# Low weight parts of the last five weight groups: formed by GpSimd in two steps instead of by VectorE in one

## The chip, the cores and the metric

The kernel runs on one core of one Trainium2 chip. The metric is the device time of one execution in microseconds. A profile of one execution shows what TensorE (PE), VectorE (DVE), ScalarE (ACT), GpSimd (POOL) and the transfer queues did.

## The reference

One encoder layer over 1024 tokens of width 1024, a grid of 16 rows by 64 columns. Cut to what matters here:

```python
h = _rmsnorm(x, norm_gain[l])
proj = h @ w_in[l]                                     # 13 groups of 256 columns
q_a, k_a, v_a, g_a, q_b, k_b, v_b, g_b = jnp.split(proj, split_at, axis=-1)
o_a = _gqa_blocked(q_a, k_a, v_a) * jax.nn.silu(g_a)   # 8 heads over all 1024 keys
o_b = _neighbourhood_attn(q_b, k_b, v_b, na_rpb[l])    # window 8 x 16, learned bias
o_b = o_b * jax.nn.silu(g_b)
x = x + jnp.concatenate([o_a, o_b], axis=-1) @ w_out[l]  # 4 more groups of 256 columns
return _rmsnorm(x, final_norm_gain)
```

## The kernel before

Everything is float32 in the reference; TensorE multiplies float16. So each operand is split into a high part (the float16 rounding) and a low part (the rest, float16 too), and a product takes three matmuls: high by high, high by low, low by high.

The weights come in 17 groups of 1024 x 256: 0 to 12 from the input projection (11 and 12 are the gate of the neighbourhood attention), 13 to 16 from the output projection. A group is loaded by a transfer that GpSimd issues (`load_w`, L212) into one of two buffers `raw`; ScalarE squares it in four quarters of 128x512 (L362); a tiny TensorE sum (L378), a VectorE step (L380) and a power on GpSimd (L381) make its scale, a column of `sm`. Then `split(g)` forms the parts, again by quarters: `hi` on ScalarE (L404, `raw` times the scale, rounded to float16) and `lo` on VectorE (L409, `raw` times the scale minus the high part). After the fourth `lo` the group counts as ready, and the load of group g + 2 into the same buffer is put on GpSimd's queue.

The program is written out slot by slot by a planner, `Flow`. One slot is one unit of attention: scores, softmax and, some slots later, the product with the values. Work beside it (evacuations, splits) waits as jobs of ScalarE and VectorE with a cost and a lateness, and each slot takes as many jobs as its budget of that engine allows (`work`). TensorE's own order takes a fixed number of projection matmuls per slot (`fill`). What is written is what each engine executes, in order: an instruction whose input is late holds everything behind it on its engine.

There are two stretches of attention. In the second, the neighbourhood attention (from about 370 us to 510 us of the span; the program marks it by `late["b"]`), there are 32 slots, four for each of the eight blocks u of 128 queries in the order 0, 7, 1, 2, 3, 4, 5, 6. In a slot TensorE writes two score tiles into two of three banks (L815, L818), VectorE adds the bias and takes the maximum (L836, tile `nm` holds the maxima), ScalarE takes the exponential twice and makes the high part (L838, L840), VectorE the low part (L845), and a transpose by DMA follows. Groups 12 to 16 are split in this stretch.

Other steps that the prediction speaks of, all in this stretch or at its border:

- The gate of the first attention: ScalarE writes tanh to `th` (L694; the only buffer of that kind, used by the second gate too), GpSimd scales it (L702), VectorE and GpSimd multiply (L703, L704). For the second gate VectorE alone reads `th` (L699).
- `narrow` (L786) on GpSimd adds the window's mask to the bias of one head, for the blocks 1 to 6, eight times in all.
- Evacuation of the values: VectorE writes `qkg` (L877, one buffer), GpSimd multiplies it into the mixed output (L879).
- The scaling of a finished block (`os`): sums on ScalarE and VectorE (L902, L907), a power on GpSimd (L910), then the high part on ScalarE (L915) and the low part on VectorE (L919), a transpose, and the output projection, whose result VectorE adds to x (L976), reloaded by transfers that GpSimd issues (L966).

Of the kernel before, what the change touches and what calls it, by code (L numbers as in the profile page):

```python
# [12 lines left out]
OP = mybir.AluOpType  # L13
# [34 lines left out]
class Flow:  # L48
# [13 lines left out]
    def at(self, delay, pos, fn, *a):  # L62
        self.due.setdefault((self.slot + delay, pos), []).append((fn, a))

    def job(self, eng, cost, fn, *a, delay=1, late=1, key=None):

        self.jobs.append((late, self.slot + delay, self.number(), eng, cost, fn, a, key))
# [75 lines left out]
def kernel(ctx: ExitStack, tc: tile.TileContext, x: bass.AP, w: bass.AP, wo: bass.AP,  # L143
# [3 lines left out]
    act, dve, pool, pe, sp = nc.scalar, nc.vector, nc.gpsimd, nc.tensor, nc.sync  # L147
# [11 lines left out]
    at, job = fl.at, fl.job  # L159
# [46 lines left out]
    raw, wp, late, x2 = {}, {}, {}, {}  # L206
# [40 lines left out]
    S_, RC, EC = 0, 17, 34  # L247
# [5 lines left out]
    def col(i, n=1):  # L253
        return sm[:, i:i + n]
# [78 lines left out]
    def alloc_wp(g):  # L333
        if g == 13:
            wp[g] = tuple(t[:, :2048].rearrange("p (k c) -> p k c", c=GC) for t in late["r"])
            return
        if g < 15:
            t = whl.tile([P, 2, KC, GC], F16, tag="whl", name=f"whl{g}")
        else:
            if g == 15:  # L340
                late["w"] = one.tile([P, 2, 2, KC, GC], F16, tag="hT0", name="whl15")
            t = late["w"][:, g - 15]
        wp[g] = (t[:, 0], t[:, 1])
# [54 lines left out]
    def split(g):  # L398

        alloc_wp(g)  # L400

        def hi(i):
            q = QUARTERS[i]
            act.activation(wp[g][0][:, q], raw[g][:, q], AF.Copy, scale=col(S_ + g))  # L404
            job("dve", 1.0 if "b" in late else 0.72, lo, i, delay=0, late=0.5 if g > 11 else 2, key=g)

        def lo(i):
            q = QUARTERS[i]
            dve.scalar_tensor_tensor(wp[g][1][:, q], raw[g][:, q], col(S_ + g), wp[g][0][:, q], op0=OP.mult, op1=OP.subtract)  # L409
            if i < 3:  # L410
                return
            ready.add(g)
            prep_e(g)
            if g + 2 < 17:
                at(1, "pre", load_w, g + 2)
            if g > 14:
                t = wraw.tile([P, 2, 1024], F32, tag="raw", name=f"x2{g}")
                for i in range(2):
                    have_x2(ORDER[2 * g - 26 + i], t[:, i])
        for i in range(4):  # L420
            job("act", 0.3 if g == 14 else 0.6, hi, i, late=0.5 if g > 11 else 2, key=g)
# [3 lines left out]
    def prep_e(g):  # L425
        dve.reciprocal(col(RC + g), col(S_ + g))
        if g < 13:
            dve.tensor_scalar(col(RC + g), col(RC + g), col(GXI), None, op0=OP.mult)
        if g in (KVA, QA, QA + 1):
            t = col(EC + g)  # L430
            dve.reciprocal(t, col(RC + g))
            dve.tensor_tensor(t, t, t, op=OP.mult)
            dve.tensor_scalar(t, t, EPS, None, op0=OP.mult)
        if g >= GATE and g < 13:
            dve.tensor_scalar(col(G2 + g - GATE), col(RC + g), 0.5, None, op0=OP.mult)
        if g == KB + 1:
            fin_scales()
        if GB <= g < 13:
            vfac(g - GB)
# [126 lines left out]
    def qa_gen(hh, up):  # L566
        def evac(pt):
            g = QA + hh
            stg = slot("stg1", [P, 2, 4, P], F16)
            a, b = (0, D) if hh == 0 else (D, 0)  # L570

            def fin(q):
                d = 4 if hh else 2
                at(d, "pre", lambda: act.activation(stg[:, :, :, a:a + D], q, AF.Copy))
                at(d, "mid", lambda: dve.tensor_tensor(stg[:, :, :, b:b + D], q, stg[:, :, :, a:a + D], op=OP.subtract))

                def tr():
                    sp.dma_start_transpose(qTa[hh][:, 2 * up:2 * up + 2].rearrange("p i h t -> p (i h) t"),
                                           stg.rearrange("p i a b -> p (i a b)"))
                at(d, "post", tr)  # L580
            norm_rope(g, up, pt, 4, 0, fin)
        yield from proj_pair(QA + hh, up, from_h, evac)

    def kva_gen(up):
        def evac(pt):
            both = slot("stg1", [P, 8, P], F16)
            stg, stg_l = both[:, :6].rearrange("p (i a) b -> p i a b", a=3), both[:, 6:]
            vs = pt[:, :, P:].rearrange("p a (h d) -> p a h d", d=D)
            at(1, "pre", lambda: act.activation(va[:, 2 * up:2 * up + 2, :, :D], vs, AF.Copy, scale=2.0 ** -14))

            def vlo():
                for i in range(2):
                    dve.scalar_tensor_tensor(va[:, 2 * up + i, :, v_lo], vs[:, i], 2.0 ** -14,
                                             va[:, 2 * up + i, :, :D], op0=OP.mult, op1=OP.subtract)
            at(1, "mid", vlo)

            def fin(k):
                def hi():
                    act.activation(stg[:, :, :2, :D], k, AF.Copy)
                    act.activation(stg[:, :, :2, D:], k, AF.Copy)  # L600
                at(2, "pre", hi)

                def lo():
                    for h, to in ((0, stg[:, :, 2]), (1, stg_l)):
                        dve.tensor_tensor(to.rearrange("p i (e d) -> p i e d", d=D),
                                          k[:, :, h, None, :].to_broadcast([P, 2, 2, D]),
                                          stg[:, :, h].rearrange("p i (e d) -> p i e d", d=D), op=OP.subtract)
                at(2, "mid", lo)

                def tr():  # L610
                    sp.dma_start_transpose(kTa[:, 2 * up:2 * up + 2].rearrange("p i a t -> p (i a) t"),
                                           both[:, :6].rearrange("p a b -> p (a b)"))
                    sp.dma_start_transpose(klo1[:, 2 * up:2 * up + 2], stg_l.rearrange("p a b -> p (a b)"))
                at(2, "post", tr)
            norm_rope(KVA, up, pt[:, :, :P], 2, 1, fin)
        yield from proj_pair(KVA, up, from_h, evac)
# [94 lines left out]
    def group(g, gens):  # L711

        def first(gen):
            prep(g + 1)
            yield from gen
        return [first(gens[0]) if g < 16 else gens[0], *gens[1:]]
# [221 lines left out]
    def have_x2(u, t):  # L938
        x2[u] = t
        if u in due:  # L940
            in_turn(load_x2, u)
# [104 lines left out]
    k, q = [kva_gen(up) for up in UP], group(1, [qa_gen(0, up) for up in UP])  # L1046
# [132 lines left out]
    a, b = ORDER[2:4]  # L1179
# [119 lines left out]
```

## Time and profile before

| | |
|---|---|
| median of 3 runs | 564.84 us (564.72 to 566.35) |
| the profiled execution | 566.36 us, of which the span is 564.5 us |
| mean granted TensorE clock | 0.977 |
| busy in the span: TensorE | 515.5 us (91%) |
| VectorE | 446.0 us (79%) |
| ScalarE | 367.8 us (65%) |
| GpSimd | 157.2 us (28%) |

The profiled execution is 1.86 us longer than its span, and 1.5 us longer than the median. A row of a timeline gives the start in us from the span's start, the duration, the engine, the line, the operation, what it writes and reads, and in brackets how long the engine stood idle before it and what ended that. Spans on GpSimd are rough.

### The profile page before, as it was taken

To read this page: it belongs to the slowest core of one execution; us is meant where nothing else is said; L and a number is where in the kernel's file an instruction comes from. 1 tells how busy PE (TensorE), PEld (TensorE's weight loads), DVE (VectorE), ACT (ScalarE), POOL (GpSimd) and SP (SyncE) were. 2 spreads that over 40 slices of the span, in tenths; PEclk is the share of its full clock that TensorE was granted. 3 is DMA by queue.
4 is the path that set the end of the run, shared out by engine and by line. 5 is a ranking of instruction groups with operands and counts; after the bars stand their busy time and mean duration, and the time that the engine had idled before them with its cause. 6 is when DMAs were issued, how large, how long until landed. Compare 5 with 4: busy or idle time off the path is not lost.

```text
span 564.5 us, 13778 instructions
## 1 busy us (share of the span) xinstructions
PE 515.5 (91%) x5583; PEld 402.4 (71%) x5583; DVE 446.0 (79%) x911; ACT 367.8 (65%) x583; POOL 157.2 (28%) x181
## 2 busy tenths in 40 slices
PE   2577989989999999999999999999998889998994
PEld 0456877767887555568888888887776667788883
DVE  4588788989887988778789887588987798988532
ACT  5546456958787759587696886367777568663211
POOL 2395887670000000000000022433821231224000
PEclk9979999999999999999999999999999998999998
DMA  8999549789999999998999899436586599996612
GB/s 242 220 181 234 122 71 210 125 143 191 203 228 174 175 216 193 193 187 173 211 197 180 189 165 214 129 68 132 105 188 105 117 255 230 181 154 139 215 38 75
DMA packets 244513, 95.47 MB, mean 169 GB/s; under 512 B 235489, under 2 KB 236001, under 8 KB 242530
## 3 DMA queue, kind: packets, MB, share of 16 engines
q1 hardware_dynamic: 240850, 73.89, 71.8%
q0 software_dynamic: 3312, 19.92, 12.2%
q8 instruction: 43, 0.70, 0.5%
q10 hardware_dynamic: 288, 0.79, 0.5%
q14 instruction: 20, 0.16, 0.1%
HBM read 29.56 MB, written 4.19 MB: 60 GB/s over the span
## 4 chain that ended last, share of the span: by engine, by line
PE 51%; DVE 9%; ACT 8%; issue 5%; DMA 4%; SPq 0%; POOL 0%; DVEq 0%; POOLq 0%; ACTq 0%
PE pj L494 19%; PE kb L494 7%; PE pjb L494 5%; PE s L725 4%; PE s L727 4%; ACT rq L838 3%; PE sb L494 3%; PE pv L758 3%; DMA ar<-ar 3%; PE pv L759 3%; PE pv L757 3%; ACT ar L840 3%; DVE ar L836 2%; DVE ar L845 2%; DMA x2b<-in_x_dram 1%
## 5 line engine op out<-in xcount | busy, mean ns | idle before, releaser
L494 PEld LDWEIGHTS <-hT 128*128 128x128 f16 x2112 | 204.9, 100 | 58.8 <-issue 16.2
L494 PE MATMUL pj<-whl,hT 128*128 128x256 f16 x1680 | 201.6, 278 | 20.9 <-DMA hT<-ar 7.8
L734 ACT ACTIVATE ar<-s,nm,sm 128x1024 f32<-128x1024 f32 x64 | 76.9, 1202 | 56.6 <-DVE nm L732 56.3
L732 DVE CUSTOM_DVE_ANT_0 ar<-s,sm 128x1024 bf16<-128x1024 f32 x64 | 82.0, 1281 | 33.9 <-PE s L727 33.6
L494 PEld LDWEIGHTS <-ar 128*128 128x128 f16 x768 | 74.6, 99 | 11.7 <-issue 2.6
L740 DVE TENSOR_TENSOR ar<-ar 128x1024 f16<-128x1024 f32 x64 | 79.5, 1242 | 1.4 <-ACT ar L735 1.4
L735 ACT ACTIVATE ar<-ar 128x1024 f16<-128x1024 f32 x64 | 67.6, 1057 | 2.1 <-DVE sum L764 0.3
L838 ACT ACTIVATE rq<-ar,nm 128x384 f32<-128x384 f32 (+1 forms) x64 | 34.1, 580 | 38.4 <-DVE nm L836 37.7
L494 PE MATMUL pjb<-whl,ar 128*128 128x256 f16 x408 | 47.4, 273 | 0.0
L494 PE MATMUL kb<-hT,whl 128*128 128x512 f16 x192 | 44.5, 379 | 0.0
L409 DVE SCALAR_TENSOR_TENSOR whl<-raw,sm,whl 128x512 f16<-128x512 f32 x52 | 38.7, 770 | 2.8 <-ACT whl L404 2.8
L758 PE MATMUL pv<-va,ar 128*128 128x64 f16 x384 | 40.1, 194 | 0.0
L757 PE MATMUL pv<-va,ar 128*128 128x65 f16 x384 | 40.1, 193 | 0.0
L759 PE MATMUL pv<-va,ar 128*128 128x65 f16 x384 | 39.9, 192 | 0.0
L757 PEld LDWEIGHTS <-ar 128*128 128x128 f16 x384 | 35.7, 97 | 5.5 <-issue 0.3
L758 PEld LDWEIGHTS <-ar 128*128 128x128 f16 x384 | 35.5, 97 | 5.5 <-issue 0.3
L725 PE MATMUL s<-kTa,rq 128*128 128x512 f16 x128 | 38.5, 383 | 0.4 <-ACT ar L734 0.4
L212 POOL DMA_DIRECT2D raw<-in_w_dram x11 | 6.7, 607 | 113.0 <-ACT ar L735 89.0
L845 DVE SCALAR_TENSOR_TENSOR ar<-rq,ar 128x768 f16<-128x768 f32 (+1 forms) x32 | 30.7, 959 | 7.9 <-ACT ar L840 7.5
L879 POOL TENSOR_TENSOR ar<-ar,qkg 128x256 f32<-128x256 f32 x16 | 18.5, 1157 | 65.0 <-DVE qkg L877 63.7
L759 PEld LDWEIGHTS <-ar 128*128 128x128 f16 x384 | 35.5, 99 | 0.0
L404 ACT ACTIVATE whl<-raw,sm 128x512 f16<-128x512 f32 x52 | 34.0, 709 | 1.4 <-POOL sm L381 1.4
(174 smaller groups left out, 978.4 us busy)
## 6 DMA issues: line engine op xcount, KB each, us to landing
raw<-in_w_dram POOLq DMA_DIRECT2D x11, 1024.0 KB, 7.7
raw<-in_wo_dram POOLq DMA_DIRECT2D x4, 1024.0 KB, 6.3
ar<-in_x_dram SPq DMA_DIRECT2D x7, 512.0 KB, 6.3
khh<-ar SPq DMA_DIRECT2D x16, 128.0 KB, 3.4
x2b<-in_x_dram POOLq DMA_DIRECT2D x4, 512.0 KB, 6.9
x<-in_x_dram POOLq DMA_DIRECT2D x4, 512.0 KB, 6.2
out_dram<-x2b SPq DMA_DIRECT2D x8, 256.0 KB, 4.2
out_dram<-x SPq DMA_DIRECT2D x7, 256.0 KB, 2.9
```

Of the source, the lines that this page charges most:

```text
L409: dve.scalar_tensor_tensor(wp[g][1][:, q], raw[g][:, q], col(S_ + g), wp[g][0][:, q], op0=OP.mult, op1=OP.subtract)
L494: pe.matmul(*o[0], **o[1])
L725: pe.matmul(s[:, c * 512:(c + 1) * 512], q, kTa[:, 4 * c:4 * c + 4, hh], start=True, stop=False)
L732: dve.tensor_tensor_reduce(out=hl[:, 1].bitcast(BF16), in0=s, in1=col(SHA).to_broadcast([P, 1024]), scale=col(NSA), scalar=3e38, op0=OP.ad ...
L734: act.activation(p32, s, AF.Exp, bias=nm, scale=col(SCA))
L735: at(0, "mid", lambda: act.activation(hl[:, 0], p32, AF.Copy))
L740: dve.tensor_tensor(hl[:, 1], p32, hl[:, 0], op=OP.subtract)
L757: pe.matmul(o, pt[:, kt], va[:, kt, hh, v_hi], start=kt == 0, stop=False)
L758: pe.matmul(o[:, :D], pt[:, kt], va[:, kt, hh, v_lo], start=False, stop=False)
L759: pe.matmul(o, pt[:, 8 + kt], va[:, kt, hh, v_hi], start=False, stop=kt == 7)
L838: act.activation(p32[:, e], t[:, e], AF.Exp, bias=nm, scale=-1.0)
L845: dve.scalar_tensor_tensor(hl[:, 1], p32, 2.0 ** 14, hl[:, 0], op0=OP.mult, op1=OP.subtract)
```

## The change

In the second stretch (`"b" in late`) `hi` no longer puts `lo` into VectorE's list of jobs; it writes it at once, and `lo` is two instructions of GpSimd: `raw` is multiplied by the scale in place, and the high part is subtracted from it. In the first stretch nothing changes. The text of the lines behind the edit moves down by 8 (L836 is L844 after).

```diff
         def hi(i):
             q = QUARTERS[i]
             act.activation(wp[g][0][:, q], raw[g][:, q], AF.Copy, scale=col(S_ + g))
-            job("dve", 1.0 if "b" in late else 0.72, lo, i, delay=0, late=0.5 if g > 11 else 2, key=g)
+            if "b" in late:
+                lo(i)
+            else:
+                job("dve", 0.72, lo, i, delay=0, late=0.5 if g > 11 else 2, key=g)
 
         def lo(i):
             q = QUARTERS[i]
-            dve.scalar_tensor_tensor(wp[g][1][:, q], raw[g][:, q], col(S_ + g), wp[g][0][:, q], op0=OP.mult, op1=OP.subtract)
+            if "b" in late:
+                pool.tensor_scalar(raw[g][:, q], raw[g][:, q], col(S_ + g), None, op0=OP.mult)
+                pool.tensor_tensor(wp[g][1][:, q], raw[g][:, q], wp[g][0][:, q], op=OP.subtract)
+            else:
+                dve.scalar_tensor_tensor(wp[g][1][:, q], raw[g][:, q], col(S_ + g), wp[g][0][:, q],
+                                         op0=OP.mult, op1=OP.subtract)
             if i < 3:
                 return
             ready.add(g)
             prep_e(g)
             if g + 2 < 17:
                 at(1, "pre", load_w, g + 2)
```

It moves instructions at three places of GpSimd's queue and one of ScalarE's.

GpSimd, at the end of the first gate: L702 and L704 belong to the gate, `raw13` and `raw14` are weight groups, `wss13` is the sum of squares of group 13, from which L381 makes its scale. Before:

```order
L704 TENSOR_TENSOR ar_78<-ar_78 128x2x256
L702 TENSOR_SCALAR ar_78<-ar_78,sm_97 128x512
L704 TENSOR_TENSOR ar_78<-ar_78 128x2x256
L381 TENSOR_TENSOR sm_97<-wss13_0_5041,mh_83 128x1
L212 DMA raw14_5427<-in_wo_dram 128x2048
L786 TENSOR_TENSOR ar_78<-ar_78,rest1_5102 128x384 x2
L879 TENSOR_TENSOR ar_78<-ar_78,qkg_85 128x256
```

The same place after; of the four pairs for group 12 (L413, L414) the last is shown, of those for group 13 the first:

```order
L413 TENSOR_SCALAR raw12_4564<-raw12_4564,sm_97 128x512
L414 TENSOR_TENSOR whl12_5280<-raw12_4564,whl12_5280 128x512
L710 TENSOR_SCALAR ar_78<-ar_78,sm_97 128x512
L712 TENSOR_TENSOR ar_78<-ar_78 128x2x256
L212 DMA raw14_5376<-in_wo_dram 128x2048
L381 TENSOR_TENSOR sm_97<-wss13_0_5041,mh_83 128x1
L413 TENSOR_SCALAR raw13_5039<-raw13_5039,sm_97 128x512
L414 TENSOR_TENSOR rest1_5102<-raw13_5039,rest0_5101 128x512
```

The four pairs of group 12 now stand ahead of the last gate step (L710 and L712, before L702 and L704), and with it ahead of the scale of group 13 and the load of group 14.

GpSimd, next, after: the last pair of group 13 and what follows (L794 is the former L786, L887 the former L879).

```order
L414 TENSOR_TENSOR rest1_5102<-raw13_5039,rest0_5101 128x512
L794 TENSOR_TENSOR ar_78<-ar_78,rest1_5102 128x384 x2
L212 DMA raw15_5503<-in_wo_dram 128x2048
L887 TENSOR_TENSOR ar_78<-ar_78,qkg_85 128x256
L794 TENSOR_TENSOR ar_78<-ar_78,rest1_5102 128x384 x2
L794 TENSOR_TENSOR rq_79<-rq_79,rest1_5102 128x384 x2
```

All eight steps of `narrow` now stand behind the four pairs of group 13, and the load of group 15 has come forward.

GpSimd, at group 14, after: `os1` is the power of block 1 (L918, the former L910), for which ScalarE's L915 waits.

```order
L413 TENSOR_SCALAR raw14_5376<-raw14_5376,sm_97 128x512
L414 TENSOR_TENSOR whl14_6044<-raw14_5376,whl14_6044 128x512
L918 TENSOR_TENSOR os1_6042<-os1_6042,mh_83 128x1
L212 DMA raw16_6159<-in_wo_dram 128x2048
L887 TENSOR_TENSOR ar_78<-ar_78,qkg_85 128x256
```

Before, the power stood right behind the evacuation of the values; now the four pairs are between them. Groups 15 (ahead of the power of block 2) and 16 (ahead of an L887) stand likewise.

ScalarE, at block 2, before: the squares of group 15 (L362, reading `raw15`) stand ahead of L915 for block 7.

```order
L838 ACTIVATE rq_79<-ar_78,nm2_5_5941 128x384
L840 ACTIVATE ar_78<-rq_79 128x768
L362 ACTIVATE rest0_5101,wss15_0_5670<-raw15_5668 128x512
L362 ACTIVATE rest0_5101,wss15_1_5671<-raw15_5668 128x512
L362 ACTIVATE rest0_5101,wss15_2_5672<-raw15_5668 128x512
L915 ACTIVATE mhl7_5887<-ar_78,os7_5886 128x512 x2
```

After:

```order
L846 ACTIVATE rq_79<-ar_78,nm2_5_5959 128x384
L848 ACTIVATE ar_78<-rq_79 128x768
L923 ACTIVATE mhl7_5899<-ar_78,os7_5898 128x512 x2
L846 ACTIVATE rq_79<-ar_78,nm2_6_6023 128x384
L846 ACTIVATE rq_79<-ar_78,nm2_7_6026 128x384
```

The squares of group 15 now stand about three slots earlier, since a group is ready, in the planner's account, as soon as ScalarE's parts are written.

## Prediction

> **What bounds the kernel now.** The split of groups 12 to 16 lies between 380 and 500 us, so I read that stretch first, by windows (columns: length, then busy time of TensorE, weight loads, VectorE, ScalarE and GpSimd with instructions, granted clock, DMA share, GB/s).
>
> ```profile
> 378.00:394.00 16.00, 15.03 (x173) 12.39 (x171) 12.90 (x31) 12.00 (x25) 5.56 (x6) 1.00 0.61 125
> 394.00:405.00 11.00, 10.27 (x113) 7.92 (x112) 10.08 (x27) 8.03 (x15) 8.22 (x7) 1.00 0.51 99
> ...
> 432.00:448.00 16.00, 10.93 (x121) 7.95 (x118) 12.93 (x31) 8.00 (x15) 4.13 (x5) 0.89 0.51 103
> 448.00:466.00 18.00, 16.15 (x190) 12.97 (x190) 16.48 (x43) 12.38 (x21) 5.35 (x8) 1.00 1.11 243
> ```
>
> TensorE is nearly full but for 432 to 448 us, VectorE is second, GpSimd is busy a quarter to a third of the time, except at 394 to 405 (8.22 of 11). Second, TensorE's waits from 378 to 530 us (total, times, longest):
>
> ```profile
> PE sb L815 <- DVE nm L836: 9.1, 6, 2.7
> ...
> PE pvb L865 <- DVE qkg L877: 1.5, 2, 0.8
> ...
> PE sb L494 <- DVE whl L409: 0.3, 1, 0.3
> ```
>
> So 9.1 + 1.5 + 0.3 = 10.9 us is all that a lighter VectorE could win here. VectorE itself stops for ScalarE or GpSimd at several places, so a delay on either passes on to TensorE.
>
> **The change part by part. Removed:** twenty VectorE instructions.
>
> ```profile
> L409 DVE SCALAR_TENSOR_TENSOR whl<-raw,sm,whl 128x512 f16<-128x512 f32 x16 | 11.6, 745 | 2.8 <-ACT whl L404 2.8
> ...
> L702 POOL TENSOR_SCALAR ar<-ar,sm 128x512 f32<-128x512 f32 x8 | 5.5, 692 | 43.4 <-ACT ar L694 43.3
> ...
> L311 POOL TENSOR_TENSOR ar<-ar 128x1024 f16<-128x1024 f32 x1 | 3.0, 3015 | 2.5 <-ACT ar L307 2.5
> ```
>
> The row has sixteen of them; the four of group 13 write another tile in the same form. 20 x 0.745 = 14.9 us leave VectorE, with the 10.9 us above as cap. **Added:** twenty pairs on GpSimd. The first half is L702's form, 0.69 us; the second is L311's kind (float32 minus float16 into float16) at half the length, 3.015 / 2 = 1.51. A pair is 2.2 us, a group 8.8 us, five groups 44 us. Bounds: the gate's pair, below, runs from 381.40 to 383.90, 2.5 us a pair and 10.0 a group; the shortest two-input step of this size took 1.27, giving 1.96 and 7.8. I take 8.8.
>
> ```profile
> L704 POOL TENSOR_TENSOR ar<-ar x8: 1272/1569/1717, 330.2 to 382.2; 128x512 f32<-128x512 f32 x8
> ...
> 381.40 0.69 POOL L702 TENSOR_SCALAR ar<-ar,sm 128x512 f32<-128x512 f32 x1 [4.60 <-ACT ar L694]
> ...
> 382.18 1.72 POOL L704 TENSOR_TENSOR ar<-ar 128x512 f32<-128x512 f32 x1
> ...
> 388.11 2.40 DVE L487 TENSOR_TENSOR vf<-sm 128x1 f32<-128x1 f32 x1
> ...
> 388.53 1.96 POOL L786 TENSOR_TENSOR ar<-ar,rest 128x384 f32<-128x384 f32 x2
> ...
> 400.12 1.38 DVE L845 SCALAR_TENSOR_TENSOR ar<-rq,ar 128x768 f16<-128x768 f32 x1 [0.29 <-ACT ar L840]
> ...
> 408.04 0.99 DVE L845 SCALAR_TENSOR_TENSOR ar<-rq,ar 128x768 f16<-128x768 f32 x1
> ```
>
> GpSimd and VectorE also hinder each other: L487, one element wide, took 2.40 us and ended as the two L786 ended; L845 took 1.38 beside two more of them, 0.99 away from them. I add about 0.7 us to a group for each long VectorE step that comes between its pairs.
>
> The Trainium skill, "SBUF — State Buffer", section "SBUF: two separate sides", speaks against the change: a VectorE operation with two SBUF inputs and a GpSimd operation that reads SBUF take one port pair by an exclusive lock, and the later one waits for the whole instruction. The trace agrees (2.40 us for L487). By that rule alone the relief would shrink; the rival "contention" prices it from rows.
>
> **Moved: what is queued behind the pairs.** GpSimd executes in order, so I walk its new queue, with the times of the trace for everything not delayed.
>
> *Groups 12 and 13.* ScalarE's and VectorE's rows, and TensorE's next score tiles:
>
> ```profile
> 381.20 0.71 ACT L404 ACTIVATE whl<-raw,sm 128x512 f16<-128x512 f32 x1
> ...
> 383.28 1.93 ACT L404 ACTIVATE whl<-raw,sm 128x512 f16<-128x512 f32 x3
> ...
> 386.18 0.55 POOL L381 TENSOR_TENSOR sm<-wss,mh 128x1 f32<-128x1 f32 x1 [2.28 <-DVE wss L380]
> ...
> 388.07 0.67 ACT L694 ACTIVATE ar<-pjb,sm 128x512 f32<-128x512 f32 x1
> ...
> 388.64 0.71 ACT L404 ACTIVATE rest<-raw,sm 128x512 f16<-128x512 f32 x1
> ...
> 391.81 0.91 ACT L838 ACTIVATE rq<-ar,nm 128x256 f32<-128x256 f32 x2 [2.46 <-DVE nm L836]
> ...
> 397.38 0.60 DVE L836 CUSTOM_DVE_ANT_0 ar<-sb,ar,sm 128x384 f32<-128x384 f32 x1
> ...
> 399.76 0.49 PE L815 MATMUL sb<-khh,qTb 128*128 128x384 f16 x2
> ```
>
> Group 12 can start at 381.9, when the first high part is there, and ends at 381.9 + 8.8 + 2 x 0.7 = 392.1. Only then come the last gate steps (0.69 + 1.27, to 394.1), the load of group 14 (0.6) and L381 for group 13 (0.55, to 395.3). ScalarE's next L694 overwrites the only `th`, so it waits until 394.1 instead of running at 388.07; behind it L404 of group 13 waits for its scale, to 396.0. The L838 behind both moves from 391.81 to 396.0: **+4.2 us**. Group 13 then takes 396.0 to 404.8, and the first `narrow`, 1.0 us long, ends near 406. L836 at 397.38 is the first that needs the narrowed bias: it moves to 406.2, **+8.8 in all**. TensorE is stopped when a score bank is not released: it wrote the tile that needs this bank at 399.76 + 0.24 = 400.0, and the bank was free at 397.98, so 2.0 us of slack leave 6.8; the following heads wait for their own `narrow` steps, with L879 and a load between them. I take **+7.5**, between 6.8 and 8.8. The VectorE relief of eight L409 does not count here, because VectorE is waiting.
>
> *Group 14* (four engines' rows in order of time; in brackets the idle time before a row and what ended it):
>
> ```profile
> 424.56 0.61 ACT L362 ACTIVATE rest<-raw 128x512 bf16<-128x512 f32 x1
> ...
> 430.50 0.69 DVE L699 SCALAR_TENSOR_TENSOR ar<-ar,pjb 128x512 f32<-128x512 f32 x1 [3.62 <-ACT ar L694]
> ...
> 435.31 0.32 PE L815 MATMUL sb<-khh,qTb 128*128 128x384 f16 x1 [2.33 <-DVE nm L836]
> ...
> 436.74 1.01 POOL L910 TENSOR_TENSOR os<-os,mh 128x1 f32<-128x1 f32 x1 [3.49 <-DVE os L909]
> ...
> 437.26 1.32 ACT L404 ACTIVATE whl<-raw,sm 128x512 f16<-128x512 f32 x2
> ...
> 439.09 1.32 ACT L915 ACTIVATE mhl<-ar,os 128x512 f16<-128x512 f32 x2
> ...
> 442.91 0.69 DVE L699 SCALAR_TENSOR_TENSOR ar<-ar,pjb 128x512 f32<-128x512 f32 x1 [2.97 <-ACT ar L694]
> ...
> 447.71 0.32 PE L815 MATMUL sb<-khh,qTb 128*128 128x384 f16 x1 [2.74 <-DVE nm L836]
> ```
>
> A gain first: three squares of group 15 (from 424.56, 2.1 us) leave the ScalarE stretch for which VectorE waited 3.62 us and then TensorE 2.33. They go to a place where ScalarE waits for VectorE, so they cost nothing there: **-2.0**. Then the loss: the last two pairs cannot start before 437.9, half of the two L404; they end at 437.9 + 4.4 + 0.5 = 442.8, and L910, which stood at 436.74, at 443.4. L915 waits for it, 439.09 to 443.4, and behind L915 stand L838 and the L694 for which VectorE already waits at 442.91, and for VectorE TensorE at 447.71. No slack is left in this chain: **+4.3**.
>
> *Group 15*, where the high part of block 2 (L915) and the low part behind it (L919) hang on the power L910:
>
> ```profile
> 457.39 1.93 ACT L404 ACTIVATE whl<-raw,sm 128x512 f16<-128x512 f32 x3
> ...
> 459.23 1.32 ACT L915 ACTIVATE mhl<-ar,os 128x512 f16<-128x512 f32 x2
> ...
> 462.85 1.88 DVE L919 SCALAR_TENSOR_TENSOR mhl<-ar,os,mhl 128x512 f16<-128x512 f32 x2
> ...
> 466.31 0.32 PE L815 MATMUL sb<-khh,qTb 128*128 128x384 f16 x1 [1.88 <-DVE nm L836]
> ```
>
> Three pairs from 458.1: 458.1 + 6.6 + 0.7, then L910: 466.0. L915 slips 6.8 us, to 467.3 at its end; L919 needs its output and slips from 462.85 to 467.3, **+4.5**, and TensorE, which waits for the L836 behind it, at 466.31. With pairs of 1.96 it would be 3.8, with 2.5 us 5.4.
>
> *Group 16*, whose four high parts ScalarE now makes in one slot, from 480.9:
>
> ```profile
> 480.96 1.17 POOL L879 TENSOR_TENSOR ar<-ar,qkg 128x256 f32<-128x256 f32 x1 [2.05 <-DVE qkg L877]
> ...
> 490.89 0.42 DVE L877 TENSOR_TENSOR qkg<-pvb,sumb 128x256 f32<-128x256 f32 x1
> ```
>
> No power is behind these pairs, but an L879: from 481.5, 8.8 + 1.4 + 1.2 = 492.9. The next L877 overwrites `qkg` and waits from 490.89, +2.0. VectorE comes there earlier, since three L409 (3 x 0.75 us) before it are gone, and I count 0.5 of that as regained on TensorE: **+1.5**. It lies between 0, if all of the 2.2 us is regained, and 2.0.
>
> *Clock.* In 432 to 448 us the granted clock is 0.89 over 16 us, 1.8 us lost, after TensorE idled 2.33. The new stalls are as long; I add one such loss, **+1.7**, between 0 and 5.
>
> Sum: 7.5 - 2.0 + 4.3 + 4.5 + 1.5 + 1.7 = +17.5. Behind 500 us TensorE is full and passes it on. The profiled execution's 566.36 becomes 583.9; the median lies 1.5 below that execution, so 582.
>
> **The rivals.**
>
> *Mild:* the price at its lower end (7.8 a group, no contention) and only the first block on the path, the others absorbed where VectorE has been relieved: +7.5 - 2.0 + 1 to 4, near 572. For it speaks that VectorE gains 14.9 us and that a planner's slots after a stall could run denser; against it that TensorE's waits at 447.71 and 466.31 end on exactly the chains that L910 holds.
>
> *Faster:* GpSimd's idle time hides the pairs and TensorE's waits on VectorE fall by half of 10.9: 559 to 561. It decides if no L910, L381 or `narrow` stands behind a group when its reader is due; the new queue shows that they do.
>
> *Contention:* the queue costs little, but each of the twenty pairs holds up VectorE by half a step of 1.1 us on average, 11 us, which eats the 14.9: no change, 563 to 566.
>
> *Heavy:* pairs of 2.5 us and more, stretched by VectorE, and several clock losses: over 590, near 596.
>
> **How the numbers follow.** Forecast (+10 to +24): 0.62; mild (+4 to +10): 0.18; faster: 0.10; contention 0.04; heavy 0.06. A measurement tells about 0.3% (1.7 us) from no change. So slower 0.86, same 0.04, faster 0.10. The forecast's own range is 574 to 588; with most of the mild case and the edge of the heavy one 570 to 590.
>
> **What would show it.** Right: ScalarE idle at the L694 near 388 and at the L915 of blocks 1 and 2, released by GpSimd; L836 near 400 waiting for L786; GpSimd busy without a gap from 382 to about 415; TensorE idle of 4 us and more near 396 and 404; busy time of GpSimd up by 44 us or more. Wrong: these waits missing, TensorE's waits on L836 smaller than 9.1 us, or a pair well under 2 us, which would make every term smaller.

## The result and the profile after

The change made the kernel slower: 600.71 us median (598.65 to 602.55, 4 runs) against 565.60 us (564.72 to 566.85, 4 runs) for the kernel before, a ratio of 1.059 with a 95% interval of 1.055 to 1.063. Here and below, medians and ranges hold every run, while ratios and intervals leave out a run that took over 1.5% longer than the fastest of its kernel. That is +35 us; the forecast was +17.5 us and its range ended at 590 us. The direction held; the rise that was forecast is half of the one that came.

The page of the kernel after, its span and its busy times:

```profile
span 599.5 us, 13793 instructions
...
PE 523.7 (87%) x5583; PEld 405.7 (68%) x5583; DVE 435.4 (73%) x891; ACT 368.1 (61%) x583; POOL 210.1 (35%) x221
```

GpSimd's busy time rose by 52.9 us (157.2 before), VectorE's fell by 10.6 us (446.0 before), although twenty steps of 0.745 us, 14.9 us, had left it. TensorE executes the same 5583 matmuls in 8.2 us more (523.7 against 515.5), at a lower mean granted clock (0.958 against 0.977).

TensorE's waits from 378 to 560 us (total, times, longest):

```profile
PE sb L823 <- DVE nm L844: 28.3, 6, 10.8
PE pvb L873 <- DVE qkg L885: 6.2, 4, 2.4
PE sb L502 <- POOL whl L414: 3.9, 2, 2.2
PE pvb L873 <- DMA ar<-ar: 0.4, 1, 0.4
```

Together 38.8 us. The same view of before gives 9.1 + 1.5 + 0.3 and 1.4 for a transfer, 12.3 us. So 26.5 us are new waits, 8.2 us are the slower matmuls, and this is 34.7 of the 35.0 us by which the span grew.

What made VectorE late stands in the waits of ScalarE and VectorE, 378 to 600 us; the first fence is ScalarE, the second VectorE:

```profile
ACT mhl L923 <- POOL os L918: 19.6, 6, 8.0
...
ACT ar L702 <- POOL ar L712: 9.4, 1, 9.4
```

```profile
DVE ar L707 <- ACT ar L702: 12.0, 2, 9.9
...
DVE ar L844 <- POOL ar L794: 7.9, 2, 7.6
DVE mhl L927 <- ACT mhl L923: 6.4, 1, 6.4
```

Three of these end on an instruction of GpSimd that stands behind pairs: the power of a finished block (L918), the last gate step (L712), the narrowed bias (L794). The other two, VectorE's longest waits for ScalarE's L702 and L923 (9.9 and 6.4 us), come right behind ScalarE's own waits for that power (6.90 and 8.02 us). The lengths of the new instructions, first by line (shortest, median, longest, in ns), then as groups:

```profile
L413 POOL TENSOR_SCALAR raw<-raw,sm x20: 1553/1563/2000, 382.3 to 522.5; 128x512 f32<-128x512 f32 x20
```

```profile
L414 POOL TENSOR_TENSOR whl<-raw,whl 128x512 f16<-128x512 f32 x16 | 20.4, 1275 | 1.3
L710 POOL TENSOR_SCALAR ar<-ar,sm 128x512 f32<-128x512 f32 x8 | 5.5, 690 | 38.8 <-ACT ar L702 38.7
```

The scaling took 1.56 us, never less than 1.55, where the gate's scaling (L710) of the same tile shape takes 0.69. The subtraction took 1.28 in the mean. A stretch of the timeline shows pairs back to back:

```profile
388.64 1.56 POOL L413 TENSOR_SCALAR raw<-raw,sm 128x512 f32<-128x512 f32 x1
390.28 1.15 POOL L414 TENSOR_TENSOR whl<-raw,whl 128x512 f16<-128x512 f32 x1
391.41 1.56 POOL L413 TENSOR_SCALAR raw<-raw,sm 128x512 f32<-128x512 f32 x1
```

From start to start 2.77 us. Beside other work the pairs were longer: the four of group 12 ran from 382.27 to 394.20 us, 11.9 us and not 8.8. Where TensorE stood, in four rows of its timeline:

```profile
388.70 1.23 PE L502 MATMUL sb<-whl,hT 128*128 128x256 f16 x5 [2.20 <-POOL whl L414]
...
411.90 0.32 PE L823 MATMUL sb<-khh,qTb 128*128 128x384 f16 x1 [3.98 <-DVE nm L844]
...
470.38 0.48 PE L823 MATMUL sb<-khh,qTb 128*128 128x384 f16 x1 [10.84 <-DVE nm L844]
...
495.07 0.48 PE L823 MATMUL sb<-khh,qTb 128*128 128x384 f16 x1 [6.80 <-DVE nm L844]
```

And the clock that was granted around them, by windows (the column before the last two):

```profile
394.00:420.00 26.00, 17.13 (x144) 12.53 (x144) 10.98 (x24) 11.38 (x22) 21.95 (x21) 0.87 0.38 108
420.00:448.00 28.00, 26.41 (x311) 20.81 (x311) 22.41 (x58) 24.04 (x47) 8.83 (x11) 1.00 0.69 114
448.00:470.00 22.00, 10.23 (x126) 8.14 (x125) 11.41 (x26) 7.14 (x12) 15.71 (x13) 0.86 0.58 122
470.00:496.00 26.00, 18.82 (x194) 13.86 (x194) 16.61 (x45) 15.13 (x28) 15.62 (x15) 0.83 0.80 146
```

In the windows with long stalls the clock is 0.83 to 0.87, in 420 to 448 us, where no stall is over 1 us, it is 1.00. Finer windows show that a stall is paid for behind it: the clock was 0.57 in 402 to 406 us, 0.51 in 470 to 474, 0.50 in 496 to 500 and 0.57 in 528 to 532, in each case right behind a stall of 2 us or more. The Trainium skill, "TensorE: Matmul & The Clock Gate", section "Why this matters for your kernels", asks for no idle gaps of TensorE over about 3 us between bursts; the rows agree for the long gaps, but length alone doesn't sort the short ones: the kernel before lost clock behind gaps of 2.33 us (0.57 in 436 to 440 us) and 1.88 us (0.61 in 466 to 470) and none behind one of 2.74 us (1.00 in 448 to 452).

### The profile page after: what moved, and what is told of

Its sections match the earlier page's. It is cut to its first block, busy times and chain, and to the rows that moved or that the text cites. A ratio compares the mean times of both kernels' runs of the same rounds, so it can differ in the third digit from the quotient of the medians.

```text
span 599.5 us, 13793 instructions
## 1 busy us (share of the span) xinstructions
PE 523.7 (87%) x5583; PEld 405.7 (68%) x5583; DVE 435.4 (73%) x891; ACT 368.1 (61%) x583; POOL 210.1 (35%) x221
## 3 DMA queue, kind: packets, MB, share of 16 engines
q0 software_dynamic: 3312, 19.92, 11.6%
## 4 chain that ended last, share of the span: by engine, by line
PE 49%; POOL 11%; issue 7%; DVE 5%; ACT 4%; DMA 4%; POOLq 0%; DVEq 0%; ACTq 0%
PE pj L502 18%; PE kb L502 7%; POOL raw L413 5%; PE pjb L502 4%; PE s L733 4%; PE s L735 4%; DMA ar<-ar 4%; PE sb L502 3%; POOL whl L414 3%; PE pv L766 3%; PE pv L767 2%; PE pv L765 2%; DVE ar L844 2%; ACT rq L846 1%; ACT ar L848 1%
## 5 line engine op out<-in xcount | busy, mean ns | idle before, releaser
L502 PEld LDWEIGHTS <-hT 128*128 128x128 f16 x2112 | 205.8, 100 | 64.5 <-issue 21.2
L502 PEld LDWEIGHTS <-ar 128*128 128x128 f16 x768 | 76.5, 101 | 13.3 <-issue 2.4
L853 DVE SCALAR_TENSOR_TENSOR ar<-rq,ar 128x768 f16<-128x768 f32 (+1 forms) x32 | 33.5, 1047 | 20.7 <-ACT ar L848 20.5
L823 PE MATMUL sb<-khh,qTb 128*128 128x384 f16 (+1 forms) x64 | 16.6, 327 | 28.3 <-DVE nm L844 28.3
L765 PEld LDWEIGHTS <-ar 128*128 128x128 f16 x384 | 35.7, 97 | 5.5 <-issue 0.3
L766 PEld LDWEIGHTS <-ar 128*128 128x128 f16 x384 | 35.4, 97 | 5.5 <-issue 0.3
L413 POOL TENSOR_SCALAR raw<-raw,sm 128x512 f32<-128x512 f32 x20 | 32.8, 1638 | 11.3 <-ACT whl L404 5.7
L381 POOL TENSOR_TENSOR sm<-wss,mh 128x1 f32<-128x1 f32 x17 | 10.6, 621 | 74.4 <-DVE wss L380 74.4
L502 PE MATMUL pjb<-whl,hT 128*128 128x256 f16 x288 | 36.4, 286 | 0.0
```

The source lines that it names most:

```text
L413: pool.tensor_scalar(raw[g][:, q], raw[g][:, q], col(S_ + g), None, op0=OP.mult)
L502: pe.matmul(*o[0], **o[1])
L765: pe.matmul(o, pt[:, kt], va[:, kt, hh, v_hi], start=kt == 0, stop=False)
L766: pe.matmul(o[:, :D], pt[:, kt], va[:, kt, hh, v_lo], start=False, stop=False)
L853: dve.scalar_tensor_tensor(hl[:, 1], p32, 2.0 ** 14, hl[:, 0], op0=OP.mult, op1=OP.subtract)
```

## The experiments

The theory after the result was: what costs is the place of the pairs in GpSimd's order, times their length; behind them wait L712, L794 and L918, on which ScalarE, VectorE and so TensorE hang. The rivals: only the length of the pairs matters; or the contention of GpSimd with VectorE for memory.

### The scaling in two operations

```diff
-pool.tensor_scalar(raw[g][:, q], raw[g][:, q], col(S_ + g), None, op0=OP.mult)
+pool.tensor_scalar(raw[g][:, q], raw[g][:, q], 0.0, col(S_ + g), op0=OP.add, op1=OP.mult)
```

> The changed kernel, with the scaling on GpSimd written in the form that the gate uses (add 0.0, then times the column), so the same values. Theory 'price in the queue': the one-operation scaling took 1.56 us where the gate's two-operation form takes 0.69; with it a pair falls from 2.77 to about 2.0 us, a group from 11.2 to 8, each of the five delays by about 3 us, and the time lands at 578 to 586. Rival 'size alone': the price is that of 512 columns read from the raw tile and not of the form; the scaling stays at 1.56 and the time at 598 to 602. Rival 'contention': as many GpSimd steps hold up VectorE as before, so not more than 3 us are gained, 596 to 600.

587.90 us (587.51 to 588.27, 4 runs), ratio to before 1.037 (1.032 to 1.042). Its group of scalings, and ScalarE's wait for the power:

```profile
L413 POOL TENSOR_SCALAR raw<-raw,sm 128x512 f32<-128x512 f32 x20 | 16.6, 831 | 13.7 <-ACT whl L404 7.8 <-issue 4.6 <-ACT rest L404 0.9
```

```profile
ACT mhl L923 <- POOL os L918: 11.6, 5, 5.3
```

One more operation in the instruction halved it, 1638 to 831 ns in the mean. Twenty times 0.8 us is 16 us of GpSimd, and the excess over before fell from 35 to 21 us: the program gets back most of the length that the pairs lost. The time lies 2 us above the band of the price theory and 8 us and more below the others.

### What makes the scaling slow

Each of the four quarters of a group got another form (L414, L416, L418 and L420, in this order). The fourth takes a constant 1.5 in place of the scale, so that the low parts of that quarter are not those of the reference.

```diff
+                if i == 0:
+                    pool.tensor_scalar(raw[g][:, q], raw[g][:, q], col(S_ + g), None, op0=OP.mult)
+                elif i == 1:
+                    pool.tensor_scalar(raw[g][:, q], raw[g][:, q], 0.0, col(S_ + g), op0=OP.add, op1=OP.mult)
+                elif i == 2:
+                    pool.tensor_scalar(raw[g][:, q], raw[g][:, q], col(S_ + g), 0.0, op0=OP.mult, op1=OP.add)
+                else:
+                    pool.tensor_scalar(raw[g][:, q], raw[g][:, q], 1.5, None, op0=OP.mult)
```

> The changed kernel with a different form of the scaling in each quarter: times the column alone; add 0.0 then times the column; times the column then add 0.0; times the constant 1.5 alone (in that quarter the scale is left out, so the low parts are not the reference's). Theory 'a column as first operand is slow': 1.56, 0.69, 1.56, 0.69 us. Rival 'one operation alone is slow': 1.56, 0.69, 0.69, 1.56. Rival 'size alone': 1.56 four times. Time between 585 and 600.

596.36 us, one run. The four lines (shortest, median, longest, in ns):

```profile
L414 POOL TENSOR_SCALAR raw<-raw,sm x5: 1567/1597/1997, 385.1 to 509.8; 128x512 f32<-128x512 f32 x5
```

```profile
L416 POOL TENSOR_SCALAR raw<-raw,sm x5: 681/696/1122, 388.2 to 513.0; 128x512 f32<-128x512 f32 x5
```

```profile
L418 POOL TENSOR_SCALAR raw<-raw,sm x5: 688/1118/1394, 390.1 to 514.9; 128x512 f32<-128x512 f32 x5
```

```profile
L420 POOL TENSOR_SCALAR raw<-raw x5: 1489/1491/1492, 392.4 to 517.5; 128x512 f32<-128x512 f32 x5
```

A single multiplication is the slow form, whether by a column (1.57) or by a constant (1.49). Two operations take 0.68 and 0.69 us at best in the two orders; the medians of 0.70 and 1.12 are five instructions each at different places of the program, and don't tell the orders apart. Why one operation costs more than two, no run shows.

### Half of the groups at a time

```diff
-if "b" in late:
+if "b" in late and g < 14:
```

In `hi` and in `lo`; the other kernel has `g > 13` there. The remaining low parts stay jobs of VectorE.

> Only groups 12 and 13 on GpSimd, 14 to 16 on VectorE as before. Theory 'queue': the stalls behind these two groups (gate buffer, scale of group 13, narrowing of the bias) cost TensorE 11.6 us and some clock: 577 to 582, with the first two stalls as in the changed kernel and none of the later ones. Rival 'contention': 8 of 20 pairs, spread over the whole stretch: +14, without a stall that ends on GpSimd.

> Only groups 14 to 16 on GpSimd. Theory 'queue': ScalarE waits for the powers of blocks 1 and 2 behind the pairs (6.9 and 8.0 us in the changed kernel) and VectorE for the buffer of the values: 581 to 587; with the run of groups 12 and 13 the two excesses add up to the 35 us of the change, within 3. Rival 'relief': where only weights that are needed late are formed on GpSimd, VectorE's relief shows: 562 to 568.

Groups 12 and 13 alone: 582.79 us (580.15 and 585.42), ratio 1.028 (1.019 to 1.036). Groups 14 to 16 alone: 586.34 us (585.16 and 587.52), ratio 1.034 (1.027 to 1.041). The first lies 0.8 us above its queue band, the second in it. The excesses of 16.1 and 19.7 us add up to 35.8, the whole change's 35.1, though the two runs of the first differ by 5 us. Within that spread nothing is handed from the first two groups to the later ones, and each half has its own chain. Of the first, VectorE's wait for the narrowed bias; of the second, ScalarE's for the power:

```profile
DVE ar L844 <- POOL ar L794: 7.9, 2, 7.6
```

```profile
ACT mhl L923 <- POOL os L918: 17.9, 4, 7.9
```

### Group 12 alone, group 13 alone

> The pairs of group 12 alone on GpSimd, as in the change; all other low parts on VectorE. With groups 12 and 13 there the excess is 17 us (e2_g12_13, 582.8). Late low part and queue: TensorE waits for the low part itself (2.2 and 1.7 us) and for L885 behind L702, which stands behind L712 and the pairs (2.2 us), some 6 us, and L381 of group 13 comes some 10 us later than before; with the lower clock behind the stalls 572 to 577 us. Work as such: half of 17 us, 573 to 575 us, but without L702's wait of 9.4 us for L712 and without L502's waits for L414.

> The pairs of group 13 alone on GpSimd, as in the change. Queue: the narrowed rows (L794) wait behind four pairs of 2.8 us, begin near 399 us where they began at 388.5 us, and VectorE's L844 waits for them; group 13's low part itself is not yet needed, so the loss is the 1 to 4 us of that wait on TensorE: 567 to 572 us. If the first block's loss in the prediction (all of it by the narrowed rows) holds: 572 to 575 us. Work as such: half of e2's 17 us, 573 to 575 us, without a wait for L794.

Group 13 alone: 574.60 us (574.01 to 575.32, 3 runs) beside 569.18 us for before, ratio 1.010 (1.005 to 1.016), +5.4 us. In its timeline TensorE stands at

```profile
401.54 0.48 PE L823 MATMUL sb<-khh,qTb 128*128 128x384 f16 x1 [4.34 <-DVE nm L844]
...
409.70 0.19 PE L873 MATMUL pvb<-ar 128*128 128x65 f16 x1 [1.59 <-DVE qkg L885]
```

The first row is the wait for the narrowed bias, the chain that the prediction walked. The time lies above the 567 to 572 us of the queue theory; it fits the band in which all of the first block's loss comes by the narrowed rows (572 to 575) and equally that of the work as such (573 to 575), but the latter was to come without a wait for L794, and VectorE waited 6.8 us for it. Group 12 alone: 571.44 us in one run, below both of its bands (572 to 577 and 573 to 575); the other two took 581.7 and 581.9, and in the profile, which is of one of these, the first high part of group 12 is made 4.0 us later than in the kernel before, ahead of any pair, so only the stalls at the edit are read from it:

```profile
392.44 0.71 PE L502 MATMUL sb<-whl,hT 128*128 128x256 f16 x5 [2.19 <-POOL whl L414]
395.22 0.81 PE L502 MATMUL sb<-whl,hT 128*128 128x256 f16 x6 [1.06 <-POOL whl L414]
...
407.01 0.19 PE L873 MATMUL pvb<-rq,ar 128*128 128x65 f16 x1 [1.93 <-DVE qkg L885]
```

TensorE waits for the low part of group 12 itself (a third time at 398.00 us, 1.96 us). No wait for a narrowed row is among them, as the queue theory had it. TensorE's stalls in this stretch are 5.3 us more than before with group 12 alone and 5.5 us with group 13 alone, together near the 11.6 us of the whole change. But whether group 12's share in the time is 2 us (this one run against 569.2) or the 10.7 that are left of 16.1 once group 13's 5.4 are taken off, these runs don't settle.

### The narrowed bias on VectorE

```diff
-pool.tensor_tensor(bias[hh][:, h4i], bias[hh][:, h4i], late["inner"], op=OP.add)
+dve.tensor_tensor(bias[hh][:, h4i], bias[hh][:, h4i], late["inner"], op=OP.add)
```

> The whole change, but the eight narrowed bias rows (L794, 128x384) are added by VectorE, in VectorE's own order, so that no score waits for a row that stands behind GpSimd's pairs. Place in the queue: VectorE's wait of 7.6 us for L794 at 411 us is gone, L702's wait of 9.4 us for L712 stays, and TensorE's waits for L844 in the first block fall by 4 to 6 us; 8 more VectorE rows of some 0.5 us give 0 to 2 us back: 594 to 599 us. Contention or size alone: 600 to 604 us, the wait taken over by VectorE's own added work.

595.13 us (593.45 and 596.81, 2 runs) beside 567.84 us, ratio 1.049 (1.043 to 1.056): an excess of 27.3 us where the whole change has 35.1, in the band of the queue theory. VectorE's wait for L794 is gone, TensorE's wait for VectorE's L844 fell from 28.3 to 24.1 us:

```profile
PE sb L823 <- DVE nm L844: 24.1, 5, 10.8
```

So with the pairs as long as ever, taking eight short instructions out from behind two groups of them gave some 5 to 8 us back, though VectorE had more to do. That is the queue's signature and not the lengths'.

### The same pairs, one per slot

Groups 14 to 16 on GpSimd in the same two instructions as in the change, but as jobs of a list of their own, from which one pair is issued at the end of each slot, behind the power (L919 in this kernel) and the evacuation (L888) of that slot.

```diff
-            self.budget = {"act": us - self.base[1], "dve": us - self.base[2]}
+            self.budget = {"act": us - self.base[1], "dve": us - self.base[2], "pool": 1.0}
...
             last()
+        self.work("pool")
         self.run("end")
...
+            if g > 13:
+                job("pool", 1.0, lo, i, delay=0, late=2, key=g)
```

> Only the order on GpSimd differs from e3_14_16 (586.3 us): groups 14 to 16 on GpSimd in the same two instructions of the same length, groups 12 and 13 on VectorE, but a pair is issued at the end of a slot, one per slot, behind that slot's L918 and L888, instead of four pairs wherever ScalarE's high parts stand. Place in the queue decides: L923's wait for L918, 17.9 us in 4 rows of e3, falls to one pair of 2.8 us at most in each of the three blocks, and 568 to 574 us are measured. Contention for the memory port, or the instructions as such, decide: GpSimd and VectorE run the same work for as long, and 583 to 588 us stay.

577.51 us (577.14 to 580.36, 3 runs) beside 567.84 us, ratio 1.020 (1.015 to 1.025): an excess of 9.7 us where the same groups in the order of the change have 19.7. ScalarE's wait for the power fell from 17.9 us to

```profile
ACT mhl L924 <- POOL os L919: 1.5, 2, 0.8
```

The instructions are the same and as many, so half of the excess was the place. The time falls between the two bands, and the other half is not left at the old places. TensorE's rows of this kernel:

```profile
489.85 0.32 PE L824 MATMUL sb<-khh,qTb 128*128 128x384 f16 x1 [1.10 <-DVE nm L845]
...
501.94 1.44 PE L503 MATMUL sb<-whl,ar 128*128 128x256 f16 x6 [4.86 <-POOL whl L415]
```

The kernel before has the first of these rows at 489.23 us. Up to here, with eight of the twelve pairs done, the program is 0.6 us later, and 1.4 us of lateness it had already ahead of the first pair (382.64 against 381.20 us for the first high part of group 12); the loss comes at 497 to 511 us, where TensorE waits for group 16's parts. The same in two operations, and with group 13 added:

> As e6_spaced, with the scaling written as two operations (add 0.0, times the column), 0.69 us when nothing else runs. Place in the queue: 564 to 569 us, the waits of L923 for L918 below 2 us each; below 565 only if the 0.8 us pieces that VectorE is relieved of stood on the path. Contention: 576 to 582 us (the e3 excess of 19.7 us less the third or so that the shorter form gave back in e1_twoop).

> As e8_spaced_two, with group 13 on GpSimd too, its four pairs one per slot between the narrowed bias rows (L795) and L888; group 12 alone stays on VectorE. Place in the queue: one pair of about 2.1 us stands ahead of a narrowed row, no L712 waits behind a pair, so the first block costs 0 to 4 us over e8_spaced_two: 564 to 573 us. Contention, or an excess of the first block that comes from group 13's work as such: 574 to 584 us.

Groups 14 to 16: 576.42 us (575.89 to 578.64, 4 runs), ratio 1.016 (1.012 to 1.020); with group 13: 580.67 us (579.41 to 583.01, 4 runs), ratio 1.024 (1.020 to 1.029). Both lie in the bands given to contention or to the work as such, not in those of the queue. What group 13 adds, 4.3 us, no run takes apart. But in groups 14 to 16 the loss is not spread over the pairs. TensorE's largest new wait is one of 4.6 us for a low part (L415), and its reason stands in GpSimd's rows, first of the kernel before, then of groups 14 to 16 in two operations, one per slot:

```profile
450.08 0.55 POOL L212 DMA_DIRECT2D raw<-in_wo_dram  x1 [1.77 <-ACT ar L840]
...
478.37 0.54 POOL L381 TENSOR_TENSOR sm<-wss,mh 128x1 f32<-128x1 f32 x1 [1.16 <-DVE wss L380]
```

```profile
460.19 1.16 POOL L415 TENSOR_TENSOR whl<-raw,whl 128x512 f16<-128x512 f32 x1
...
461.86 0.59 POOL L213 DMA_DIRECT2D raw<-in_wo_dram  x1
...
494.38 0.56 POOL L382 TENSOR_TENSOR sm<-wss,mh 128x1 f32<-128x1 f32 x1 [4.75 <-DVE wss L381]
```

Group 16 is loaded into the buffer that group 14 leaves. The last pair of group 14, now spread over four slots, ended at 461 us, the load was issued at 461.86 instead of 450.08 us, and the scale of group 16 followed at 494.38 instead of 478.37 us. Of these 11.8 and 16.0 us, 3.7 are no effect of the edit, since this profile lay as far behind ahead of the first pair (384.87 against 381.20 us for the first high part of group 12); 8.1 and 12.3 us are left. The low parts of group 16 then came when TensorE already wanted them. The place had been mended and a new chain made.

### The load brought forward again

Two ways, both with the scaling in two operations: two pairs a slot for groups 14 to 16 (the diff), or one pair a slot and group 14 back on VectorE (`g > 14` in place of `g > 13`).

```diff
-"pool": 1.0}
+"pool": 2.0}
```

> As e8_spaced_two (groups 14 to 16), but two pairs may be issued per slot: group 14's four pairs end one to two slots earlier, and with them the load of group 16 into its rows. Late load: the load is issued 3 to 6 us earlier than in e8, and the time lies at 566 to 573 us, between e8 and e10, with L503's wait for L415 near 500 us below 3 us. The work of the pairs as such: 575 to 578 us as e8, since the same instructions run.

> Groups 15 and 16 only on GpSimd, one pair per slot, scaling in two operations; group 14 back on VectorE, so that its raw rows are free as early as before and group 16 is loaded into them near 450 us as before (in e8_spaced_two: L213 at 461.9 us, 8 us later beside the 4 us by which that profile lies behind). Late load: the 6 to 8 us of TensorE's waits near 500 us (L503 for L415 and for L405, with the clock of 0.90 behind them) go, and 564 to 568 us are measured. The work of the pairs as such (port, VectorE stretched), spread over the groups: two thirds of e8's excess of 9.1 us stay, 570 to 574 us.

Two a slot: 573.09 us (568.59 to 579.39, 10 runs), ratio 1.008 (1.004 to 1.012). Groups 15 and 16: 572.48 us (569.19 to 582.88, 10 runs), ratio 1.009 (1.005 to 1.014). Before, measured beside them: 567.50 us. With two a slot the load is issued at 450.76 us, and TensorE's waits from 420 to 530 us are

```profile
PE sb L824 <- DVE nm L845: 8.4, 5, 3.2
PE pvb L874 <- DMA ar<-ar: 5.0, 2, 3.5
```

No wait for a low part is left, and the ratio fell from 1.016 to 1.008 with the same twelve pairs; the time is at the upper edge of what the late load had been given (566 to 573). The two intervals only just meet at 1.012. The 8.4 us are what the kernel before has there too (8.2); new is a transpose that came 3.5 us late, and why it did no run shows. The other kernel landed above the band of the late load (564 to 568), in that of the work as such (570 to 574): the load is early, but one pair a slot is too slow for group 16, whose last two pairs stand behind the power, and TensorE waits

```profile
PE sb L503 <- POOL whl L415: 3.9, 3, 2.5
```

So the late load was a part of what the spaced kernels lose, and some 5 us stay that it doesn't explain. No version of the change that was run beats the kernel before.

### What contention is worth

VectorE's busy time with groups 14 to 16 on GpSimd, two pairs a slot:

```profile
PE 518.3 (91%) x5583; PEld 403.4 (71%) x5583; DVE 441.5 (77%) x899; ACT 367.6 (64%) x583; POOL 181.7 (32%) x205
```

Twelve steps, 8.9 us, left VectorE and its busy time fell by 4.5 us: half of the relief is eaten by longer steps. Yet TensorE's wait for VectorE stands at 8.4 against 8.2 us. So contention isn't where the 35 us come from, and the rival falls as the main cause. It may be the reason why nothing was won; that is argued from these two figures and not shown by a run.

## Why the prediction was wrong in size

The mechanism was as forecast: what stands behind the pairs in GpSimd's order came late, and ScalarE, VectorE and TensorE with it. The sizes were off.

**The pair's price** is the term that failed: "The first half is L702's form, 0.69 us", with 2.5 us as the upper bound of a pair. L702 has two operations, the added scaling one; it took 1.56 us, and a pair 2.77, outside the bounds that the nearest rows seemed to give. The subtraction was cheaper than taken (1.28 for 1.51). The run with the scaling in two operations is the test of this: it has pairs of 0.83 + 1.27 = 2.10 us, near the 2.2 of the sum, and its excess is 21.2 us, near the +17.5; its 587.90 us lie inside the range of 570 to 590. So of the 35.1 us some 14 are this one figure.

**The clock** was the second: +1.7 taken, "between 0 and 5", and TensorE's busy time rose by 8.2 us in the change and by 6.1 us (521.6) with the scaling in two operations. At the price of the forecast, then, the clock was 4.4 us more than taken, which covers what the sum lacks against 21.2 (3.7); the new stalls of that run are 14.8 us (its four waits of 16.2, 7.2, 2.1 and 1.6 less the 12.3 of before), where 15.8 had been forecast. That the two sums come so close is partly luck: by parts these stalls are 6.4 us for groups 12 and 13, 4.5 for 14, 1.4 for 15 and 1.9 for 16, where 7.5, 2.3, 4.5 and 1.5 had been taken. In the change itself, busy time times missing clock in the windows of about 4 us behind the stalls gives an estimate of 9.9 us, at six places between 388 and 532 us, against 3.2 at two places before: the prediction counted one more such loss, and four more came, of 1.2 to 2.0 us each.

**Groups 12 and 13** (+7.5 taken; TensorE's stalls from 378 to 440 us are 14.1 us against 2.5 before, +11.6). The chain was as walked: ScalarE's L702 waited 9.35 us for the gate's L712, L381 and the narrowed rows came behind, L844 waited 7.55 us. Two things were off. The pairs were longer; and a wait had been left out: the low part of group 12 itself, two stalls of 2.20 and 1.71 us. TensorE wanted its second quarter at 386.50 us. VectorE had it ready at about 384.7 before (L409, two from 384.01 us in 1.41), and GpSimd's second pair ended at 388.65. The prediction walked the pairs of this group to their end and didn't ask when TensorE reads them. The 0.3 us for L409 that it quoted as a possible gain were no warning of this; they stand at the last low part of group 16:

```profile
494.91 2.67 PE L494 MATMUL sb<-whl,ar 128*128 128x256 f16 x23 [0.35 <-DVE whl L409]
```

Besides, the big stall came in several smaller ones (2.20, 1.71, 2.19, 3.98, 2.44 us), not as 4 us and more at two places.

**Group 14** (-2.0 + 4.3 taken; stalls at 451.64 and 470.38 us 1.31 and 10.84 us, against 2.33 and 2.74: +7.1). The gain was 1.0 us and not 2.0. The loss of the chain was right in its links and 8.1 us long: ScalarE's high part of the block waited 6.90 us for the power.

```profile
447.98 1.16 POOL L887 TENSOR_TENSOR ar<-ar,qkg 128x256 f32<-128x256 f32 x1 [5.47 <-DVE qkg L885]
449.13 2.00 POOL L413 TENSOR_SCALAR raw<-raw,sm 128x512 f32<-128x512 f32 x1
...
461.20 0.57 POOL L918 TENSOR_TENSOR os<-os,mh 128x1 f32<-128x1 f32 x1
```

The prediction let the first two pairs run ahead and counted only the last two in front of the power. In fact an evacuation (L887) that itself waited for VectorE stood ahead of the first pair, so all four ran in one row, 449.13 to 461.2 us, two of them with a scaling of 2.00 us. The third high part was ready at about 454.3 us (L404, two from 453.59 us in 1.32) and the third pair began at 455.67; that is 1.4 of the 2.6 us by which ScalarE's wait exceeds the 4.3. The last two pairs took 5.5 us and not 4.9, 0.6 more.

**Group 15** (+4.5 taken, 6.80 in its stall at 495.07 us, against 2.16 before with a small one, +4.6) came out as forecast, which is partly luck: ScalarE's wait was 8.02 us and not 6.8, and with it the prediction's own chain would have given 1.2 us more. **Group 16** (+1.5 taken) lost 4.1 us, in stalls of 1.10 and 4.31 against 1.3 before: VectorE waited 5.1 us for the L887 behind the pairs, where 2.0 had been taken.

**The rivals.** "Heavy" (over 590, near 596) has about the right time. Two of its three conditions came, pairs of more than 2.5 us and several losses of clock, but for the length it has a wrong cause: the pairs weren't stretched to it by VectorE. A scaling took 1.56 us while VectorE stood idle, and the shortest of twenty took 1553 ns.

```profile
407.44 1.56 POOL L413 TENSOR_SCALAR raw<-raw,sm 128x512 f32<-128x512 f32 x1
...
411.22 0.62 DVE L844 CUSTOM_DVE_ANT_0 ar<-sb,ar,sm 128x384 f32<-128x384 f32 x1 [7.55 <-POOL ar L794]
```

"Faster" fell where the prediction had put its condition: L918, L381 and the narrowed rows were behind a group when their readers were due. "Mild", near 572, did not come with the change as written; only kernels with fewer groups and another order came to it (572.48 and 573.09 us). "Contention" had no change in time, and the time rose by 35 us. What remains open is how the 16 us of the first block divide between group 12 and group 13, why a transpose came late with two pairs a slot, and what the last 5 us of the spaced kernels are.

## What to carry to other kernels

Before work goes to an engine because it is idle, list what stands behind it in that engine's order, and what the moved instruction's last read releases: here the place alone was worth half of the loss of groups 14 to 16, and spreading the work out to mend the place made a load late. A duration borrowed from another row holds only for the same form of instruction; where the nearest row differs in one operation, the bound has to be wider than the rows suggest. A wait of 0.3 us in the profile marks a step without slack: it was the low part of group 16, and there TensorE waited 4 to 7 us in four of the five spaced kernels. But a step without a wait can be nearly as tight, as that of group 12 was, so ask of every moved step when its reader wants it.

## What the runs showed of the hardware

- A GpSimd multiplication of a float32 tile of 128x512 in place took 1.56 us as a single operation with a column, 1.49 with a constant, and 0.69 us (0.83 in the mean of twenty) when an operation that changes nothing was added to the instruction. The Trainium skill, "GPSIMD Engine Reference", section "4.1 Engine selection", sets GpSimd against VectorE for elementwise work and has one-input work on it at "roughly line-rate". VectorE's steps on tiles of this shape took 0.68 us (L711) and 0.74 us (L409); measured by these, the form with two operations fits that, the form with one doesn't.
- A VectorE step can be held up through several GpSimd instructions. L853, 0.93 us when GpSimd was idle, took 3.75 us while four narrowed rows ran on GpSimd; the scaling took 2.00 us at its longest, where VectorE ran beside it.

```profile
414.36 3.75 DVE L853 SCALAR_TENSOR_TENSOR ar<-rq,ar 128x768 f16<-128x768 f32 x1 [0.96 <-ACT ar L848]
...
468.85 0.93 DVE L853 SCALAR_TENSOR_TENSOR ar<-rq,ar 128x768 f16<-128x768 f32 x1
```

- The granted clock was low behind stalls of TensorE and came back after some 4 to 6 us of work: 0.51 in 470 to 474 us behind the stall of 10.8 us and 1.00 in 474 to 478; 0.50 in 496 to 500 behind that of 6.8, 0.85 in 500 to 504 and 1.00 in 504 to 510. Not every stall of over 2 us cost clock: behind the one of 2.44 us it was 1.00 (418 to 422).
